# The first feed-forward's normed activation: four parts of a tile in pieces of 320 columns instead of 272

## The chip, the cores and the metric

The kernel runs on one core of a Trainium2 chip. Its time is that of one execution on the device, in microseconds (us), and what is compared is the median of several executions. The profile shows TensorE as PE (matmuls) and PEld (its weight loads), VectorE as DVE, ScalarE as ACT, GpSimd as POOL and SyncE as SP.

## What is computed

The reference is one decoder layer on 256 tokens with 16 learned meta tokens in front, so 272 columns in all: a feed-forward, two mixers side by side (attention and a short convolution), and a second feed-forward. The change is in the first feed-forward, which is

```
s = jnp.concatenate([meta, x], axis=1)            # 272 tokens of 2048
h = rms_norm(s, norm_ffn1[layer])
s = s + 0.5 * swiglu_ffn(h, ffn1_w_gu[layer], ffn1_w_down[layer])

def swiglu_ffn(h, w_gu, w_down):
    gate, up = jnp.split(h @ w_gu, 2, axis=-1)    # 2 x 5632 columns
    return (jax.nn.silu(gate) * up) @ w_down
```

All is float32.

## The kernel before

Activations lie with their features on the 128 partitions and their tokens along the free dimension, in chunks of 128 features: 16 chunks for a width of 2048. To keep float32's precision at a faster matmul type, each operand is split into a rounded part (hi, or wh for weights) and the rest (lo, or wl), and a product is three matmuls that add into one PSUM bank: hi by wh (line 329), lo by wh (line 330), hi by wl (line 331). The weights are the stationary operand of these three lines, the activation is the one that is streamed, 272 columns of it.

The class `Act` holds such a split activation. A tile of it has four parts along each partition: chunk 2g hi, chunk 2g lo, chunk 2g+1 hi, chunk 2g+1 lo. In most activations the four parts are packed, 272 columns (1088 bytes) each. Slots named in `wide_slots` come from the tag "big", whose tiles have 4 x 320 = 1280 columns. Where `piece` is given, each part takes `piece` columns of such a slot and its data lie in the last of them: `lead` = 320 - 272 = 48 columns stay free ahead of each part. `part` and `both` add that lead to every access, so no code elsewhere knows of it.

`h1`, the normed input of the first feed-forward (line 667), has all of its eight tiles in big slots, but no `piece`: its parts are packed 272 columns each and the last 192 columns of a slot lie unused. `h2`, the input of the mixers (line 733), takes the same eight slots once h1 is done with, in pieces of 320. In the program as built all of these slots begin at the same address modulo 256 bytes, and so do the weight tiles wh and wl.

`gain_split` (line 197) writes h1: for each chunk one ScalarE instruction for hi (line 201) and one VectorE instruction for lo (line 202). For h1 this is done inside the first gate product, chunk by chunk as the input arrives (`prep` and `before1`).

`linear` runs the products that read it. One call makes 4 x 128 output features from all 16 chunks: for each block of two chunks ScalarE casts the weights to wh (line 313), VectorE subtracts to wl (line 318), and TensorE runs 2 x 4 x 3 = 24 matmuls into four banks. `gate_up` calls it for the gate columns (tiles named pg) and the up columns (pu) in turn, 11 times each: 6 pairs, then the down products (pd, which read m, an activation with packed parts) of that half, 5 pairs, and the down products of the other half. Later the products named k and v read all 272 columns of h2 through the same lines of `linear`. What comes in from memory is queued on SP, as many blocks ahead as there are buffers.

Of the kernel before, what the change touches and what calls it, by code (L numbers as in the profile page):

```python
# [19 lines left out]
T = SEQ + NMETA  # L20
F = 5632
DC = D // P
# [3 lines left out]
NH = 8  # L26
# [10 lines left out]
PIECE = 320  # L37
# [19 lines left out]
def decoder_layer(ctx: ExitStack, tc: tile.TileContext, t, out):  # L57
# [606 lines left out]
        nc.vector.tensor_sub(tl[:, :, 1, :], f, tl[:, :, 0, :].bitcast(F32))  # L664


    h1 = Act("h1", DC, T, range(NH))
    norm1 = Norm(0, "1")

    pm, split_of, turned = [], [], []  # L670
# [515 lines left out]
```

## Time and profile before

| | |
|---|---|
| median of 3 executions | 2170.85 us (2170.66 to 2172.34) |
| the profiled execution | 2171.01 us |
| its span, first to last instruction | 2169.2 us |
| granted TensorE clock | 0.999 of full speed |
| instructions | 33235 |

The span falls into the first feed-forward (to some 808 us), the mixers with their merge and output product (to some 1463 us), and the second feed-forward. A row of the page's groups names line, engine, operation and tiles (output <- inputs) with partitions x elements, its count, then busy us and the mean of one in ns, then the idle time just before and what ended it. Matmuls overlap in TensorE's pipeline, so one lasts longer than the distance to the next; the timeline, which lists single instructions by their start, shows that distance.

### The profile page before, as it was taken

What the parts mean: (1) busy time and instruction counts of PE and PEld (TensorE: products, weight loads), DVE (VectorE), ACT (ScalarE), POOL (GpSimd) and SP (SyncE); (2) the same over time, 40 slices, a digit from 0 to 9 for tenths busy, and PEclk for the clock granted to TensorE, in tenths of its full rate; (3) what the DMA queues carried; (4) which work ended last, traced back from release to release, by engine and by line L of the source; (5) the groups of instructions that cost most, each with busy time, mean ns of one, the idle gap of its engine ahead of it and who ended that gap; (6) DMA issues with size and microseconds to landing.
All of it is one profiled execution on the core that took longest, in us unless ns stands there. A gap on an engine that the chain in (4) does not pass through costs nothing.

```text
span 2169.2 us, 33235 instructions
## 1 busy us (share of the span) xinstructions
PE 2156.0 (99%) x13349; PEld 1952.7 (90%) x13349; DVE 1567.5 (72%) x2054; ACT 1092.1 (50%) x1379; POOL 82.9 (4%) x93
## 2 busy tenths in 40 slices
PE   9999999999999999999999999999999999999998
PEld 9999999999999998899998888888888888888886
DVE  8555554445555557867787878678999899988997
ACT  6343343333433444555545555456665566555664
POOL 0000000000000000000000000001110111012100
PEclk9999999999999999999999999999999999999999
DMA  7555555555555555554456557557886999779965
GB/s 255 175 175 175 175 178 175 175 175 175 175 175 175 170 180 180 191 173 137 141 180 205 193 195 232 195 179 235 276 254 204 282 285 276 239 220 312 281 196 155
DMA packets 205216, 440.76 MB, mean 203 GB/s; under 512 B 10557, under 2 KB 11270, under 8 KB 205062
## 3 DMA queue, kind: packets, MB, share of 16 engines
q1 hardware_dynamic: 188118, 398.13, 54.0%
q0 software_dynamic: 16480, 39.85, 8.3%
q8 instruction: 104, 1.70, 0.3%
q10 hardware_dynamic: 464, 0.66, 0.1%
q14 instruction: 50, 0.41, 0.1%
HBM read 431.26 MB, written 2.10 MB: 200 GB/s over the span
## 4 chain that ended last, share of the span: by engine, by line
PE 96%; DVE 2%; DMA 1%; ACT 1%; issue 0%; POOL 0%; SPq 0%; DVEq 0%; ACTq 0%
PE pg L524 6%; PE pg L522 6%; PE pg L523 6%; PE pu L331 4%; PE pd L331 4%; PE pd L329 4%; PE pu L329 4%; PE pu L330 4%; PE pd L330 4%; PE pg L331 4%; PE pg L329 4%; PE pg L330 4%; PE o L327 3%; PE pd L522 2%; PE pd L523 2%; PE pd L524 2%
## 5 line engine op out<-in xcount | busy, mean ns | idle before, releaser
L318 DVE TENSOR_TENSOR wl<-st,wh 128x1024 fp32r<-128x1024 f32 (+1 forms) x361 | 440.1, 1221 | 407.8 <-ACT wh L313 407.4
L313 ACT CAST wh<-st 128x1024 fp32r<-128x1024 f32 (+1 forms) x360 | 377.1, 1048 | 538.1 <-PE pd L330 143.0
L432 DVE TENSOR_TENSOR wl<-st,wh 128x1024 fp32r<-128x1024 f32 (+1 forms) x392 | 438.4, 1126 | 68.5 <-ACT wh L431 66.7
L431 ACT CAST wh<-st 128x1024 fp32r<-128x1024 f32 (+1 forms) x392 | 371.5, 973 | 215.9 <-PE pdx L523 45.1
L431 ACT CAST wh<-t 128x1024 fp32r<-128x1024 f32 x142 | 148.3, 1053 | 206.2 <-DVE t L562 135.4
L432 DVE TENSOR_TENSOR wl<-t,wh 128x1024 fp32r<-128x1024 f32 x142 | 172.7, 1224 | 57.8 <-ACT wh L431 52.8
L329 PE MATMUL pg<-h,wh 128*128 128x272 f32 x704 | 202.9, 289 | 1.0 <-ACT h L201 0.7
L329 PE MATMUL pu<-h,wh 128*128 128x272 f32 x704 | 203.1, 289 | 0.0
L329 PE MATMUL pd<-m,wh 128*128 128x272 f32 x704 | 203.0, 288 | 0.0
L331 PE MATMUL pd<-m,wl 128*128 128x272 f32 x704 | 203.0, 288 | 0.0
L331 PE MATMUL pu<-h,wl 128*128 128x272 f32 x704 | 203.0, 288 | 0.0
L330 PE MATMUL pu<-h,wh 128*128 128x272 f32 x704 | 202.4, 288 | 0.0
L330 PE MATMUL pd<-m,wh 128*128 128x272 f32 x704 | 202.4, 288 | 0.0
L330 PE MATMUL pg<-h,wh 128*128 128x272 f32 x704 | 201.9, 288 | 0.1
L331 PE MATMUL pg<-h,wl 128*128 128x272 f32 x704 | 200.9, 289 | 0.1
L524 PE MATMUL pg<-wl,h 128*128 128x512 f32 x399 | 156.2, 391 | 0.0
L523 PE MATMUL pg<-wh,h 128*128 128x512 f32 x399 | 156.2, 391 | 0.0
L522 PE MATMUL pg<-wh,h 128*128 128x512 f32 x399 | 155.5, 390 | 0.0
L329 PEld LDWEIGHTS pg<-h,wh 128*128 128x128 f32 x704 | 132.3, 188 | 1.7 <-ACT h L201 0.9
L330 PEld LDWEIGHTS pg<-h,wh 128*128 128x128 f32 x704 | 132.8, 189 | 0.3 <-DVE h L202 0.3
L330 PEld LDWEIGHTS pu<-h,wh 128*128 128x128 f32 x704 | 132.7, 189 | 0.0
L330 PEld LDWEIGHTS pd<-m,wh 128*128 128x128 f32 x704 | 132.7, 189 | 0.0
(369 smaller groups left out, 4849.3 us busy)
## 6 DMA issues: line engine op xcount, KB each, us to landing
st<-in_ffn_w_gu_dram SPq DMA_DIRECT2D x183, 512.0 KB, 6.1
st<-in_ffn_w_down_dram SPq DMA_DIRECT2D x88, 1024.0 KB, 5.2
st<-in_ffn_w_gu_dram SPq DMA_DIRECT2D x84, 1024.0 KB, 4.9
st<-in_w_in_dram SPq DMA_DIRECT2D x48, 1024.0 KB, 5.2
st<-in_w_gate_dram SPq DMA_DIRECT2D x64, 512.0 KB, 4.6
t<-in_ffn_w_gu_dram POOLq DMA_DIRECT2D x64, 512.0 KB, 7.2
st<-in_w_branch_dram SPq DMA_DIRECT2D x32, 512.0 KB, 4.9
st<-in_w_out_dram SPq DMA_DIRECT2D x16, 1024.0 KB, 5.1
```

The costliest lines, as they stand in the source:

```text
L313: nc.scalar.copy(out=wh[:, :m, :], in_=sw)
L318: nc.vector.tensor_sub(wl[:, :m, :], sw, wh[:, :m, :].bitcast(F32))
L327: nc.tensor.matmul(acc[j][:, : 2 * n], wh[:, i, f], act.both(c, t0, t1), start=first, stop=False)
L329: nc.tensor.matmul(a, wh[:, i, f], act.part(c, 0, t0, t1), start=first, stop=False)
L330: nc.tensor.matmul(a, wh[:, i, f], act.part(c, 1, t0, t1), start=False, stop=False)
L331: nc.tensor.matmul(a, wl[:, i, f], act.part(c, 0, t0, t1), start=False, stop=last)
L431: part_last[:] = [nc.scalar.copy(out=wh, in_=src).ins]
L432: part_last.append(nc.vector.tensor_sub(wl, src, wh.bitcast(F32)).ins)
L522: nc.tensor.matmul(ps[k], hi, wh, start=first, stop=False)
L523: nc.tensor.matmul(ps[k], lo, wh, start=False, stop=False)
L524: nc.tensor.matmul(ps[k], hi, wl, start=False, stop=left[k] == 0)
```

## The change

One argument more where h1 is made:

```diff
-    h1 = Act("h1", DC, T, range(NH))
+    h1 = Act("h1", DC, T, range(NH), PIECE)
```

`PIECE` is 320. The parts of an h1 tile, which began 0, 272, 544 and 816 columns into the slot, now begin at 48, 368, 688 and 1008. In bytes that is 0, 1088, 2176 and 3264 before, and 192, 1472, 2752 and 4032 after; modulo 256 it is 0, 64, 128 and 192 before, and 192 for all four after. The slots keep their size and place, every engine has the same instructions in the same order, and no other tile moves.

## The prediction

> **What bounds the kernel now.** I read the page's busy shares and its chain of waits first, then a table of stages, then the timeline of TensorE alone. The page:
>
> ```profile
> PE 2156.0 (99%) x13349; PEld 1952.7 (90%) x13349; DVE 1567.5 (72%) x2054; ACT 1092.1 (50%) x1379; POOL 82.9 (4%) x93
> ...
> PE 96%; DVE 2%; DMA 1%; ACT 1%; issue 0%; POOL 0%; SPq 0%; DVEq 0%; ACTq 0%
> ...
> L329 PE MATMUL pg<-h,wh 128*128 128x272 f32 x704 | 202.9, 289 | 1.0 <-ACT h L201 0.7 <-ACT wh L313 0.3
> L329 PE MATMUL pu<-h,wh 128*128 128x272 f32 x704 | 203.1, 289 | 0.0
> ```
>
> TensorE is busy 99% of the span and is 96% of the chain that ended last. The two rows from the costliest groups are those that read h1. Line 329 runs 704 times for the gate half (pg) and 704 times for the up half (pu); with lines 330 and 331 that makes 6 x 704 = 4224 matmuls that read h1, and no other instruction of weight does. Their mean of 289 ns is no price: matmuls overlap, and 4224 of them at 289 ns would need 1221 us, though the whole first feed-forward lasts some 800 us, its down products included. The price is the distance from one start to the next.
>
> Busy TensorE need not be working at its best, so the stages come next (columns: stretch, its length, busy us and count of each engine, granted clock, DMA share, GB/s):
>
> ```profile
> 6.00:35.40 29.40, 28.17 (x217) 26.81 (x216) 28.12 (x62) 22.14 (x43) 0.00 (x0) 1.00 0.84 292
> ...
> 60.00:300.00 240.00, 240.00 (x1914) 240.00 (x1913) 126.09 (x155) 97.72 (x112) 0.00 (x0) 1.00 0.52 177
> 300.00:420.00 120.00, 120.00 (x958) 120.00 (x958) 55.82 (x58) 42.65 (x42) 0.00 (x0) 1.00 0.52 176
> ...
> 808.00:831.00 23.00, 23.00 (x187) 22.92 (x187) 19.25 (x40) 13.50 (x20) 0.00 (x0) 1.00 0.56 182
> 973.00:1006.00 33.00, 33.00 (x264) 30.93 (x264) 25.50 (x58) 17.56 (x51) 0.00 (x0) 1.00 0.41 131
> ```
>
> The stretch from 60 to 300 us is gate and up alone. TensorE never idles there, VectorE is busy 53% of it, ScalarE 41%, the DMA engines 52%, and the clock is fully granted. Whatever a matmul's start-to-start distance (its cadence) saves there, the end gets. From 6 to 35 us, the first gate product, it is otherwise: VectorE is busy 28.12 of 29.40 us and sets the pace. The stretches at 808 and 973 us matter for what follows: they read h2, which already has pieces of 320.
>
> **The change part by part.** Nothing is added or removed on any engine and the order stays; all tiles keep their addresses. Only the four offsets at which ScalarE and VectorE write h1 and TensorE reads it differ. Before, the parts of a tile lie 0, 1088, 2176 and 3264 bytes from its start, which is 0, 64, 128 and 192 modulo 256. After, they lie at 192 + 1280 k, so at 192 modulo 256 each. So the sum needs one price: the cadence of a 272-column matmul when all parts share a phase (the address modulo 256), against its cadence now.
>
> The timeline of TensorE has both. First h1 now, an unbroken run: 186 matmuls of which these rows are the first two, two in the middle and the last two (start, then duration):
>
> ```profile
> 60.75 0.29 PE L329 MATMUL pg<-h,wh 128*128 128x272 f32 x1
> ...
> 82.35 0.29 PE L330 MATMUL pg<-h,wh 128*128 128x272 f32 x1
> 82.48 0.29 PE L331 MATMUL pg<-h,wl 128*128 128x272 f32 x1
> ...
> 83.86 0.29 PE L330 MATMUL pg<-h,wh 128*128 128x272 f32 x1
> 83.98 0.29 PE L331 MATMUL pg<-h,wl 128*128 128x272 f32 x1
> ```
>
> That is 185 steps in 83.98 - 60.75 = 23.23 us, or 125.6 ns each. Is this the layout or the stage? The down product of the same feed-forward reads another tile, m, whose pieces are 272 columns too, so its parts also take four phases. Again the first and the last of an unbroken run, 160 matmuls:
>
> ```profile
> 350.03 0.29 PE L329 MATMUL pd<-m,wh 128*128 128x272 f32 x1
> ...
> 369.99 0.29 PE L329 MATMUL pd<-m,wh 128*128 128x272 f32 x1
> ```
>
> 159 steps in 19.96 us: 125.5 ns, the same. Now h2, read by the same lines of code, at the same width, with weights prepared in the same way, from tiles that take the very slots that h1 had, in pieces of 320. First the product k, 72 matmuls, then a run of v, 35 matmuls:
>
> ```profile
> 808.45 0.29 PE L329 MATMUL k<-h,wh 128*128 128x272 f32 x1
> ...
> 817.21 0.29 PE L331 MATMUL k<-h,wl 128*128 128x272 f32 x1
> ```
> ```profile
> 980.04 0.29 PE L330 MATMUL v<-h,wh 128*128 128x272 f32 x1
> ...
> 984.24 0.29 PE L331 MATMUL v<-h,wl 128*128 128x272 f32 x1
> ```
>
> 71 steps in 8.76 us are 123.4 ns; 34 steps in 4.20 us are 123.5 ns. Starts are shown to 0.01 us, so the four cadences are good to about 0.05, 0.06, 0.14 and 0.3 ns. The common phase is therefore cheaper by 125.6 - 123.4 = 2.2 ns or 125.6 - 123.5 = 2.1 ns; I take 2.1. And h1 after the change is not merely like h2: slot, offset, width and reading lines are those of k and v.
>
> The bounds of this price: nothing at one end, if the stage and not the layout makes k quick, and 2.2 ns at the other. I stay at the upper end since the row that it goes by differs from the changed code in nothing but the name of the product and the work beside it. That work speaks for me: in k's stretch VectorE is busy 19.25 of 23 us (84%) and ScalarE 59%, more than in the gate and up stages, and k is the quicker one.
>
> One rule of the Trainium skill speaks against the change. SBUF — State Buffer, section Specifications (TRN2), gives a cacheline of 16 bytes, each cross to a new line paying a penalty. All four of the old offsets and the new one are multiples of 16 apart, and a part of 1088 bytes is 68 lines at each of them. By that rule alone nothing changes; the 125.6 against 123.4 ns above says that something beyond it counts.
>
> **The sum.** Each gate or up product is 16 chunks x 4 banks x 3 = 192 matmuls; there are 22.
> - 21 products with TensorE unbroken: 21 x 192 = 4032 matmuls x 2.1 ns = 8.5 us less.
> - The first gate product: 192 x 2.1 = 0.4 us, if TensorE set its pace. VectorE does, at 28.12 of 29.40 us, so I take 0 and keep 0.4 as a bound.
> - The writes of h1, 16 on each engine:
>
> ```profile
> L201 ACT ACTIVATE h<-s,vec x32: 492/507/525, 717.8 to 1470.0; 128x272 fp32r<-128x272 f32 x16, 128x256 fp32r<-128x256 f32 x16
> L201 ACT ACTIVATE h<-s,gain x16: 505/509/524, 6.4 to 31.0; 128x272 fp32r<-128x272 f32 x16
> ```
>
>   The second row is h1 at 509 ns in the middle, the first is h2 (and h3) at 507. I price the new offset at 0; 16 x 20 ns = 0.3 us either way bounds it, from the spread of that row.
> - Covers: quicker matmuls must still be fed. A block of 24 matmuls (3.01 us before, 2.96 after) needs one wl subtraction on VectorE and one wh cast on ScalarE; from 60 to 300 us VectorE has 114 us free and ScalarE 142. The weights must come 1.7% faster, at a DMA share of 0.52. Nothing there is late. If the cover failed and VectorE set these stages, the whole 8.5 us would be lost.
> - Later stages start 8.5 us earlier, and so do their transfers, which are issued as buffers come free and not by the clock; I price this at 0.
>
> The profiled execution took 2171.0 us, 1.8 around its span of 2169.2, against a median of 2170.85: 0.1 apart. 2171.0 - 8.5 = 2162.5 on that execution, and **2162.4 us** for the median.
>
> **Rivals.**
> - No change, 2170.9 us. The address plays no part, and k and v are quick for a reason of their own stage. For it: PEld is busy 240.00 of 240.00 us in gate and up, as if weight loads set the cadence whatever is streamed, and 30.93 of 33.00 us around v. Against it: around k PEld is busy 22.92 of 23.00 us, as full, and the cadence is 123.4; and pd shows h1's cadence under a lighter load. Chance 0.10. The cacheline rule of the Trainium skill gives the same result.
> - Half of it, 2166.7 us: part of the 2.1 ns is the stage's. If 1.05 ns is the layout's, 4032 x 1.05 = 4.2 us. The same rows speak against it. Chance 0.04.
> - Slower, 2188.6 us. Parts at four phases take turns, while parts at one phase could meet the same storage as the weight loads beside them each time, in the stages where PEld is never free. Its price is the longest step that h1 shows now: 82.35 to 82.48 is 0.13 us against a mean of 125.6. Every step at 130 ns would cost 4.4 x 4032 = 17.7 us. It decides as soon as the new cadence lies over 125.6. Against it: k, at the one phase and beside full weight loads, has 123.4. Chance 0.06.
> - That the change doesn't do what it says: a slot holds 1280 columns, four pieces of 320 exactly, and every access goes through the offset of 48 columns. I see no way for this, and give it nothing of its own.
>
> **How the numbers follow.** The forecast has 0.80. Its own range is 2161.6 to 2163.6: the price between 1.9 ns (7.7 us) and 2.2 ns (8.9 us) and the first product's 0.4. The range for 8 in 10 goes from 2161.0 to 2167.0, so that half the gain is in it; no change and slower, together 0.16, stay outside. About 0.2%, 4.3 us, is what a measurement of this kernel can tell from no change. Faster by more than that: the forecast, 0.80. Within: no change and half of it, 0.14. Slower: 0.06.
>
> **What would show it.** In the changed kernel's timeline unbroken runs of pg and pu should step by 123.4 ns, a product from the second on should last 23.7 us instead of 24.1, and pd should stay at 125.5. The down product of the first half should begin 4.5 to 5 us earlier, k 8 to 9 us earlier, and the stages behind should keep their lengths. The first gate product should still end near 35.4. A cadence of pg near 125.6 would prove me wrong in the price; a cadence of 123.4 with an end at 2171 would prove me wrong in the cover.

## The result and the profile after

| | before | the change |
|---|---|---|
| median | 2170.85 us (5 executions, 2170.31 to 2172.34) | 2161.84 us (5 executions, 2161.47 to 2162.50) |
| ratio | | 0.9959, 95% interval 0.9949 to 0.9970 |
| span of the profiled execution | 2169.2 us | 2160.0 us |

9.0 us less in the medians, 9.2 in the spans; 8.5 were forecast. First the page of the changed kernel, the rows that answer to those shown of before, and one of pd:

```profile
PE 2147.3 (99%) x13349; PEld 1943.6 (90%) x13349; DVE 1566.5 (73%) x2054; ACT 1091.2 (51%) x1379; POOL 82.8 (4%) x93
...
PE 97%; DMA 1%; DVE 1%; ACT 0%; issue 0%; POOL 0%; SPq 0%; DVEq 0%; ACTq 0%
...
L329 PE MATMUL pd<-m,wh 128*128 128x272 f32 x704 | 203.0, 288 | 0.0
...
L329 PE MATMUL pu<-h,wh 128*128 128x272 f32 x704 | 201.9, 287 | 0.0
...
L329 PE MATMUL pg<-h,wh 128*128 128x272 f32 x704 | 201.6, 287 | 0.0
```

The counts are the same and TensorE is as busy as before in share. The mean of a pg or pu matmul fell from 289 to 287 ns, that of pd stayed at 288. The stages of the changed kernel (columns as in the prediction: stretch, length, then PE, PEld, DVE, ACT, POOL, clock, DMA share, GB/s) say that the cover held:

```profile
6.00:35.40 29.40, 28.70 (x221) 27.05 (x221) 28.35 (x62) 21.81 (x43) 0.00 (x0) 1.00 0.84 292
60.00:295.00 235.00, 235.00 (x1908) 235.00 (x1907) 125.27 (x152) 97.24 (x112) 0.00 (x0) 1.00 0.53 180
```

TensorE still never idles from 60 to 295 us. The weights come at 180 GB/s where they came at 177. Now the cadence, from TensorE's timeline of the changed kernel (start, duration): the first and the last of an unbroken run of 170 matmuls of pg, the first and the last of 181 of pd, and the first of k:

```profile
61.23 0.28 PE L329 MATMUL pg<-h,wh 128*128 128x272 f32 x1
...
82.08 0.29 PE L330 MATMUL pg<-h,wh 128*128 128x272 f32 x1
...
349.78 0.28 PE L330 MATMUL pd<-m,wh 128*128 128x272 f32 x1
...
372.38 0.29 PE L330 MATMUL pd<-m,wh 128*128 128x272 f32 x1
...
799.28 0.29 PE L329 MATMUL k<-h,wh 128*128 128x272 f32 x1
```

pg: 169 steps in 20.85 us, 123.4 ns; it was 125.6. pd: 180 steps in 22.60 us, 125.6 ns, unchanged. k began at 808.45 us before and begins at 799.28 now, 9.17 us earlier. As the whole span is 9.2 us shorter, all of the gain arises ahead of k and nothing of it is lost behind. The end of the first gate product can be read from the matmul that follows it (before, then after):

```profile
36.19 0.39 PE L225 MATMUL ssq_ps<-ssq,ones 128*128 128x272 f32 x1
```
```profile
35.98 0.39 PE L225 MATMUL ssq_ps<-ssq,ones 128*128 128x272 f32 x1
```

0.21 us of the 9.17 came there. The other 8.96 over 4032 matmuls are 2.2 ns each.

### The profile page after: what moved, and what is told of

The parts are those of the page before. It is cut to its first block, busy times and chain, and to the rows that moved or that the text cites. A ratio compares the mean times of both kernels' runs of the same rounds, so it can differ in the third digit from the quotient of the medians.

```text
span 2160.0 us, 33235 instructions
## 1 busy us (share of the span) xinstructions
PE 2147.3 (99%) x13349; PEld 1943.6 (90%) x13349; DVE 1566.5 (73%) x2054; ACT 1091.2 (51%) x1379; POOL 82.8 (4%) x93
## 4 chain that ended last, share of the span: by engine, by line
PE 97%; DMA 1%; DVE 1%; ACT 0%; issue 0%; POOL 0%; SPq 0%; DVEq 0%; ACTq 0%
PE pg L522 6%; PE pg L524 6%; PE pg L523 6%; PE pd L331 4%; PE pd L329 4%; PE pd L330 4%; PE pu L329 4%; PE pu L331 4%; PE pu L330 4%; PE pg L331 4%; PE pg L329 4%; PE pg L330 4%; PE o L327 3%; PE pd L524 3%; PE pd L523 3%; PE pd L522 3%
```

## The experiments

The change altered two things at once: the four parts of a tile came to one phase (address modulo 256 bytes), and that phase became a certain one. All runs below but the last are one execution each, with its profile; what is compared is the cadence (the mean distance from start to start), which a run of 170 matmuls gives to about 0.06 ns, and the time stands beside it. Edits are shown against the change, with lines left out at the dots. Where an edit adds lines, the three matmul lines of `linear` (329 to 331) and those of the second feed-forward (522 to 524) have higher numbers in the timeline. Phases are given as the distance from the phase of the weight tiles wh and wl, so that before the change the parts lay at 0, 64, 128 and 192 bytes, and after it all at 192. Each run of matmuls below is unbroken unless the text says otherwise. That 256 bytes is the period was taken as given; no run was made to test it.

**One phase, but another one.** Where the lead of h1 is made, two runs set it by hand, to 0 and to 16 columns (distance 0 and 64):

```diff
...
+            if lead is not None:
+                self.lead = lead
...
-    h1 = Act("h1", DC, T, range(NH), PIECE)
+    h1 = Act("h1", DC, T, range(NH), PIECE, lead=0)
```

> h1 in pieces of 320 as in the change, but the data at the front of each piece: all four parts share a phase still, which is 192 bytes lower than in the change and is the phase at which the weight tiles wh and wl lie. Theory A (that the parts share a phase is what counts, whichever it is): pg and pu step by 123.3 ns, time near 2161.8 us. Rival B (the phase of the change is a good one in itself): pg and pu step by 125 ns or more, time 2169 us or more. Rival C (a phase equal to that of the weights is a bad one, the slower rival of the prediction): more than 125.6 ns, time over 2171 us.

> h1 in pieces of 320, the data 16 columns into each piece: one phase for all parts, 128 bytes below that of the change and 64 above that of the weights. Theory A: pg and pu step by 123.3 ns, 2161.8 us. Rival B: 125 ns or more, 2169 us or more. Rival C: 123.3 ns, as the phase is not that of the weights.

The timeline with a lead of 0, then of 16 columns; first and last of 170 matmuls:

```profile
61.30 0.28 PE L332 MATMUL pg<-h,wh 128*128 128x272 f32 x1
...
82.48 0.29 PE L333 MATMUL pg<-h,wl 128*128 128x272 f32 x1
```
```profile
61.31 0.29 PE L332 MATMUL pg<-h,wh 128*128 128x272 f32 x1
...
82.72 0.29 PE L333 MATMUL pg<-h,wl 128*128 128x272 f32 x1
```

169 steps in 21.18 us are 125.3 ns (2170.0 us), and in 21.41 us 126.7 ns (2175.6 us, beside 2172.1 for the kernel before on the same chip). Theory A falls: with one phase for all parts the kernel can be nearly as slow as before, or slower. Rival C, that the phase of the weights is the bad one, falls too: it asked for more than 125.6 ns there and for 123.3 at 64 bytes above, and got 125.3 and 126.7. Rival B, that the phase of the change is a good one in itself, has both runs.

**Two phases, and four dealt anew.** One run leaves hi in place and puts lo 16 columns ahead (hi 192, lo 128). Another packs h1 in 272 columns as before the change, but 48 columns into the slot:

```diff
...
-            return self.tiles[c // 2][:, c % 2, lo, self.lead + t0 : self.lead + t1]
+            l = self.lead - lo * self.back
+            return self.tiles[c // 2][:, c % 2, lo, l + t0 : l + t1]
...
-    h1 = Act("h1", DC, T, range(NH), PIECE)
+    h1 = Act("h1", DC, T, range(NH), PIECE, back=16)
```
```diff
...
-                    self.tiles.append(raw[:, : 4 * w].rearrange("p (c l w) -> p c l w", c=2, l=2))
+                    self.tiles.append(raw[:, shift : shift + 4 * w].rearrange("p (c l w) -> p c l w", c=2, l=2))
...
-    h1 = Act("h1", DC, T, range(NH), PIECE)
+    h1 = Act("h1", DC, T, range(NH), shift=48)
```

> h1 in pieces of 320; the hi parts where the change has them, the lo parts 16 columns (64 bytes) further ahead. So two phases in place of four, and of three matmuls in a row the second reads the other phase. Theory A: the step between matmuls of different phases is dearer, so pg and pu step by 124.5 to 126 ns, 2166 to 2172 us. Rival B (each matmul by its own phase): two of three keep 123.3, the third costs 125.6 or so, 124.1 ns on average, 2165 us.

> h1 packed as before the change, 272 columns each, but 48 columns into the slot: the same four phases as before, dealt to other parts (hi of the first chunk has what lo of the second had). Theory A: four phases mixed as before, 125.6 ns, 2170.9 us. Rival B: the same on average, 125.6 ns, since the four phases are the same. Should it come out near 123.3 ns (2161.8 us), neither holds, and it is the place of the first part alone that counts.

The timeline with lo 16 columns ahead, then packed and shifted, 170 matmuls each:

```profile
61.28 0.29 PE L333 MATMUL pg<-h,wl 128*128 128x272 f32 x1
...
82.32 0.28 PE L331 MATMUL pg<-h,wh 128*128 128x272 f32 x1
```
```profile
61.21 0.29 PE L331 MATMUL pg<-h,wl 128*128 128x272 f32 x1
...
82.30 0.28 PE L329 MATMUL pg<-h,wh 128*128 128x272 f32 x1
```

124.5 ns (2169.6 us) and 124.8 ns (2167.5 us). The first run's cadence alone would give some 2166 us: up to 2135 us it is 4.4 us ahead of the kernel before, and it loses 3 us of that at the end of the second feed-forward, where the granted clock is 0.66 and 0.65 from 2140 to 2150 us. Its 124.5 ns lies at the edge of what theory A had (124.5 to 126) and 0.4 above what B had. With the price that the next runs give to distance 128, 126.6 ns, two hi at 123.4 and one lo at 126.6 make 124.5. Packed and shifted, the set of phases is that of before and yet it is 0.8 ns cheaper: neither theory had that. So it counts which part lies at which phase. That hi is read twice for each time that lo is explains a part only: by the prices in the table below this deal would cost some 125.3 ns.

**The rest of the sweep.** Leads of 32 and 40 columns (distance 128 and 160), by the same edit as the first two runs:

> h1 in pieces of 320, the data 32 columns into each piece: one phase for all parts, 64 bytes below that of the change. It ends the sweep in steps of 64 bytes: so far pg and pu step by 123.3 ns in the change, 125.3 at the phase of the weights (64 bytes above the change's), 126.7 at 64 bytes above the weights. Theory D (each phase has its own price, and four mixed phases cost near the mean of theirs): the mix of before, 125.55, is a sixth of twice 125.3, 126.7, twice this phase and 123.3, so this phase costs 126.3 ns and the time is near 2174 us. Rival E (only the phase of the weights and the one above it are bad): 123.3 to 124.5 ns, 2162 to 2166 us.

> h1 in pieces of 320, the data 40 columns into each piece: one phase, 32 bytes below that of the change, and so, unlike all others tried, at a multiple of 64 bytes (128 modulo 256). If the price goes smoothly with the phase: between the change's 123.3 ns and that of 32 columns, some 124 to 125. If it is full 64-byte rows that count (1088 bytes are 17 rows from here and 18 from the others): less than 123.3, perhaps 122, 2156 us.

```profile
61.29 0.29 PE L332 MATMUL pg<-h,wh 128*128 128x272 f32 x1
...
82.69 0.29 PE L333 MATMUL pg<-h,wl 128*128 128x272 f32 x1
```
```profile
61.24 0.29 PE L332 MATMUL pg<-h,wh 128*128 128x272 f32 x1
...
82.09 0.28 PE L333 MATMUL pg<-h,wl 128*128 128x272 f32 x1
```

The timeline with 32 columns gives 126.6 ns (2175.6 us), that with 40 columns 123.4 ns (2162.4 us). So theory D has the first, 0.3 ns off. The second is neither a mean of its neighbours nor quicker than the change: neither theory of that run, full rows of 64 bytes or a smooth course, had it.

| distance of the streamed parts from the weights, bytes | 0 | 64 | 128 | 160 | 192 |
|---|---|---|---|---|---|
| cadence of 272 columns, ns | 125.3 | 126.7 | 126.6 | 123.4 | 123.4 |

**To the weights, or by itself?** Padding of 32 and of 64 bytes behind the constants moves all other tiles together, the weights too:

```diff
     fr = const.tile([P, 2, 4], F32, name="fr")
+    const.tile([P, 8], F32, name="pad")
```

> The change, with 32 bytes of padding ahead of all tiles but the constants: h1 begins at 0 modulo 64 and the weights wh and wl at 0 modulo 256, while h1 lies to the weights as in the change. If the phase of h1 to the weights decides: pg and pu 123.3 ns as in the change, all other products as they are, 2161.8 us. If the phase of the streamed tile by itself decides: another cadence for pg and pu, and other cadences in the later stages too.

> The change, with 64 bytes of padding ahead of all tiles but the constants: h1 lies at the phase that had 125.3 ns with 0 columns of lead, while it lies to the weights as in the change. If the phase of h1 to the weights decides: 123.3 ns, and the other products as they are, 2161.8 us. If the phase of the streamed tile by itself decides: pg and pu 125.3 ns, 2170 us for these alone.

The timeline with 32 bytes of padding, then with 64, again 170 matmuls:

```profile
61.29 0.28 PE L330 MATMUL pg<-h,wh 128*128 128x272 f32 x1
...
82.13 0.29 PE L331 MATMUL pg<-h,wl 128*128 128x272 f32 x1
```
```profile
61.21 0.29 PE L331 MATMUL pg<-h,wl 128*128 128x272 f32 x1
...
82.06 0.28 PE L329 MATMUL pg<-h,wh 128*128 128x272 f32 x1
```

123.3 and 123.4 ns (2162.6 and 2163.2 us). With 64 bytes of padding h1 lies at the phase that cost 125.3 ns with a lead of 0, and it doesn't cost that. For these products the distance between the streamed tile and the stationary one decides, not the address of either.

One product does not follow. The output product o streams 512 columns of an activation (hi and lo of 256) against wh and then 256 against wl, and its operands too keep their distance in the padded runs. The first and the last of its 512 matmuls (four calls of `linear`, with a few matmuls of other products in between), in the change and then with 32 bytes of padding:

```profile
1361.13 0.39 PE L327 MATMUL o<-mg,wh 128*128 128x512 f32 x1
...
1453.50 0.28 PE L331 MATMUL o<-mg,wl 128*128 128x256 f32 x1
```
```profile
1361.45 0.39 PE L327 MATMUL o<-mg,wh 128*128 128x512 f32 x1
...
1454.82 0.28 PE L331 MATMUL o<-mg,wl 128*128 128x256 f32 x1
```

That is 92.37 us and 93.37; with 64 bytes of padding it is 93.29, and in the kernel before and every run that alters h1 or m alone it is 92.37. So for o something besides the distance modulo 256 counts, the address or another thing that the padding moved; no run tells which. It is about what the two padded runs take longer than the change (0.7 and 1.3 us).

**Everywhere?** Three kernels put a gap between the weights and all activations and shorten the lead of h1 and h2 by as much, so that these stay where they were to the weights (24 columns are 96 bytes; 16 and 48 in the other two):

```diff
...
+    apool.tile([P, 24], F32, tag="gap", bufs=1, name="gap")
...
-            self.width, self.lead = width, 0 if piece is None else piece - width
+            self.width, self.lead = width, 0 if piece is None else piece - width - 24
```

> As the run with a gap of 96 bytes, but 64, with the lead shortened by 16 columns. Packed activations keep the four phases 0, 64, 128 and 192 to the weights, dealt anew: hi of a tile's first chunk at 64, its lo at 128, hi of the second at 192, its lo at 0. Priced by the uniform runs (125.3, 126.7, 126.7 and 123.3 ns at 0, 64, 128 and 192), pd is (2 x 126.7 + 126.7 + 2 x 123.3 + 125.3) / 6 = 125.3 ns against 125.55, some 0.5 us less. In the 512-column products the streamed weights lie 64 bytes below the stationary activation, as h1 lies to the weights in the change. Theory F: they get cheaper than 227 ns, each ns being near 4 us. Rival G: 227 ns, 2161 us in all.

> The change, with a gap of 96 bytes between the weight tiles and all activations, and the lead of h1 and h2 shortened by 24 columns, so that these lie to the weights as in the change. Packed activations move to 32, 96, 160 and 224 bytes past the phase of the weights; those that are stationary in the 512-column products move to 96. Theory F (the phase of the streamed operand to the stationary one decides, everywhere): pg, pu, k and v keep 123.4 ns; pd leaves 125.55 and, if its new phases all cost what 160 bytes cost in the run with 40 columns (123.4), comes to 123.4, 4.6 us less in all; and the 512-column products leave their 227 ns, either way. Rival G (only 272-column products feel it): pd moves, the 512-column products keep 227 ns.

> As the run with a gap of 96 bytes, but 192, with no lead left. Packed activations have the four phases as hi 192, lo 0, hi 64, lo 128 to the weights: pd is (2 x 123.3 + 125.3 + 2 x 126.7 + 126.7) / 6 = 125.3 ns by the uniform runs. In the 512-column products the streamed weights lie 64 bytes above the stationary activation, where h1 had its worst cadence. Theory F: they get dearer than 227 ns. Rival G: 227 ns.

The timelines with gaps of 64, 96 and 192 bytes, in each the first and the last of 181 matmuls of pd, then of an unbroken run of 512-column matmuls in the second feed-forward (130, 127 and 132 of them), where the weights are streamed and the activation is stationary:

```profile
349.80 0.29 PE L333 MATMUL pd<-m,wl 128*128 128x272 f32 x1
...
372.25 0.28 PE L333 MATMUL pd<-m,wl 128*128 128x272 f32 x1
...
1599.68 0.39 PE L526 MATMUL pg<-wl,sp 128*128 128x512 f32 x1
...
1629.77 0.39 PE L526 MATMUL pg<-wl,sp 128*128 128x512 f32 x1
```
```profile
349.78 0.29 PE L331 MATMUL pd<-m,wh 128*128 128x272 f32 x1
...
372.28 0.29 PE L331 MATMUL pd<-m,wh 128*128 128x272 f32 x1
...
1600.36 0.40 PE L525 MATMUL pg<-wh,sp 128*128 128x512 f32 x1
...
1629.84 0.39 PE L525 MATMUL pg<-wh,sp 128*128 128x512 f32 x1
```
```profile
349.78 0.29 PE L332 MATMUL pd<-m,wh 128*128 128x272 f32 x1
...
372.23 0.29 PE L332 MATMUL pd<-m,wh 128*128 128x272 f32 x1
...
1599.72 0.39 PE L526 MATMUL pg<-wl,sp 128*128 128x512 f32 x1
...
1629.99 0.40 PE L525 MATMUL pd<-wh,m 128*128 128x512 f32 x1
```

And the same stretch of the change itself, 134 such matmuls with the operands at one phase:

```profile
1599.83 0.39 PE L524 MATMUL pgx<-wl,h 128*128 128x512 f32 x1
...
1629.97 0.39 PE L522 MATMUL pdx<-wh,m 128*128 128x512 f32 x1
```

| gap, bytes | 0 (the change) | 64 | 96 | 192 |
|---|---|---|---|---|
| pd, 272 columns, ns | 125.6 | 124.7 | 125.0 | 124.7 |
| distance of the streamed weights from the stationary activation, bytes | 0 | 192 | 160 | 64 |
| 512 columns, ns | 226.6 | 233.3 | 234.0 | 231.1 |
| time, us | 2161.8 | 2182.5 | 2186.0 | 2173.7 |

Rival G falls: the 512-column products feel it too, by 4 to 7 ns, and with some 3400 of them the kernel takes 12 to 24 us longer. The kept traces hold two controls. The products gx and qx in the mixers also have 512 columns, but their stationary operand is h2, whose distance the gaps leave alone: they keep 226.5 to 227.0 ns in all three runs. And with 64 bytes of padding, where the activations of the second feed-forward move as with the gap of 64 but the weights move too, pg of that stage keeps its 227.1 ns, against 233.2 with the gap. But theory F had the sign wrong for the gap of 64, and its condition for the gap of 96, that all new distances cost what 160 does, did not hold: pd came to 125.0 ns and not 123.4. 64 bytes below the stationary tile (distance 192) is a good place for 272 streamed columns and a bad one for 512 columns of weights. Of the distances tried, these do best at 0, where the kernel had them. pd did better than the uniform prices say (124.7 where they give 125.3), so prices of single phases add up only roughly.

**A version that uses it.** m has no room for pieces of 320: its tiles fill their slots. But the deal of its parts to the four phases can be altered inside the tile, to the one that the gaps of 64 and 192 had shown to be cheaper:

```diff
...
-            return self.tiles[c // 2][:, c % 2, lo, self.lead + t0 : self.lead + t1]
+            k = c % 2
+            if self.dealt:
+                k, lo = ((0, 1), (1, 0), (1, 1), (0, 0))[2 * k + lo]
+            return self.tiles[c // 2][:, k, lo, self.lead + t0 : self.lead + t1]
...
+            if act.dealt:
+                nc.scalar.copy(out=tl[:, :, 1, :], in_=f)
+                for i in range(2):
+                    nc.vector.tensor_sub(tl[:, 1 - i, 0, :], f[:, i, :], tl[:, i, 1, :].bitcast(F32))
+                continue
...
-        m = Act("m", len(half) * GC, n)
+        m = Act("m", len(half) * GC, n, dealt=True)
```

> The change, and the four packed parts of m, which pd reads, dealt anew within their tile, with nothing moved or widened: to the weights hi of the first chunk lies at 64, its lo at 128, hi of the second at 192, its lo at 0. pd had 125.55 ns so far; with this deal it had 124.7 in the runs with a gap of 64 and of 192 bytes, and pg and pu the same in the run of h1 packed and shifted. Theory F (phases to the weights, and their order): pd 124.7 ns, 2112 x 0.83 = 1.75 us less than the change: 2160.1 us, and 0.9951 of before. Rival: the gap runs had it from the place of other tiles; then pd stays at 125.55 and the time at 2161.8. The lo parts take two VectorE instructions in place of one, 22 more in all, in stages in which VectorE is busy about half the time: nothing.

Its timeline, 181 matmuls of pd:

```profile
349.81 0.29 PE L338 MATMUL pd<-m,wh 128*128 128x272 f32 x1
...
372.26 0.28 PE L338 MATMUL pd<-m,wh 128*128 128x272 f32 x1
```

180 steps in 22.45 us, 124.7 ns. The median of 5 executions is 2160.05 us (2159.90 to 2161.92) against 2171.34 for the kernel before; ratio 0.9951, interval 0.9938 to 0.9965. The spans are 2158.3 us here and 2160.0 for the change. The ratios' intervals overlap; what tells this kernel from the change is the cadence, 0.85 ns x 2112 matmuls = 1.8 us.

## Why the prediction was right, and where its reason was not

- *TensorE's cadence sets the first feed-forward.* Right: TensorE has no idle time from 60 to 295 us after the change, and all of the gain is there ahead of k.
- *The price.* Read from k (2.2 ns) and from v (2.1 ns), taken as 2.1, measured as 2.2. The run of v was the shorter of the two, 35 matmuls against 72, and good to 0.3 ns only; k alone would have given 8.9 us. This makes most of the 0.7 us between forecast and result in the spans; the next point is most of the rest. Of the signs that the prediction listed, the down product of the first half began 4.9 us earlier (4.5 to 5 were said) and k 9.2 (8 to 9 were said).
- *The first gate product.* Taken as 0 with a bound of 0.4; it gave 0.21 us. VectorE sets its pace, as it was busy 28.35 of 29.40 us there after the change, but not for the whole of it. The prediction's end of this product near 35.4 us was read off a window that is too short: it ends at 36.19 before and at 35.98 after.
- *The writes of h1 and the stages behind.* As priced: a write of hi takes 508 ns where it took 509 (medians), and the span moved by what k's start moved by.
- *The reason.* "The common phase is therefore cheaper" was wrong. Of the five common phases tried, one costs 125.3 ns, hardly less than the mix of before (125.6), and two cost more, 126.6 and 126.7. What held the number up is another sentence of the prediction, that slot, offset, width and reading lines were those of k and v: h2 (made in line 723, not 733) lies 192 bytes from the weights, and the change put h1 there. As far as the stated reason goes it was luck that the common phase was a cheap one: for h1 led by 16 or 32 columns instead of 48 the argument from "one phase" forecasts a gain, and these runs took 2175.6 us, some 4 us more than the kernel before.
- *The slower rival.* A common phase that is slower than the mix exists, at distances of 64 and 128 bytes, with 126.7 ns rather than the 130 it was priced at; at the distance of the change it does not. Whether streamed parts and weight loads meet in the same storage there, as the rival had it, no run shows; at the phase of the weights themselves, distance 0, the cadence is 125.3.
- *No change.* That the address plays no part was wrong: the same pg matmuls step by 123.4 ns where they stepped by 125.6. The page SBUF — State Buffer of the Trainium skill, section Specifications (TRN2), counts cachelines of 16 bytes, and all offsets tried are multiples of 16 bytes apart. The runs differ by 3.3 ns among them, so that rule is not the whole account. The same page, section SBUF: two separate sides, lets only VectorE's and GpSimd's shared ports cause contention among the engines. No run here bears on that rule: what the runs show, a cadence that depends on where two operands lie to each other, is within one engine.

What inside the chip makes one distance dear and another cheap was not found, nor why the order of distances differs between 272 streamed columns and 512, nor what makes o dearer in the padded runs; no run separated the width from the roles of weights and activation.

## What to carry to other kernels

Where TensorE never idles, read the distance from start to start of its matmuls in an unbroken run, per product: a difference of 2 ns between two products of the same shape is a lead that costs no instruction to follow. Try the start of the streamed tile at several offsets to the stationary one modulo 256 bytes, and take the measured best for each shape; one offset for all is no rule, and a gap that helps one product, as it did pd, can cost the others more. When a forecast is carried over from a twin in the same kernel, list everything that the twin shares with the changed code, since the thing named as the cause may not be the one that acts.

## What the runs showed of the hardware

- The cadence of 272-column matmuls depends on the distance, modulo 256 bytes, of the streamed operand from the stationary one: 123.4 ns at 160 and 192, 125.3 at 0, 126.7 at 64, 126.6 at 128. Moving both together by 32 or 64 bytes did not change it (123.3 and 123.4).
- With 512 columns of weights streamed it is 226.6 ns at one phase, and 231.1, 233.3 and 234.0 ns with the stationary tiles 192, 64 and 96 bytes further on. Moving both by 64 bytes did not change it (227.1 for pg of the second feed-forward).
- The distance is not all in every product: the 512 matmuls of o took 92.37 us, and 93.37 and 93.29 with both operands moved by 32 and 64 bytes.
- With operands at several phases, it counts as well which part lies at which: the same four phases gave 125.6 ns in one deal and 124.7 in another.
